# Rounded-type transposes for two tiles of each change of stage and for B's values, and a VectorE sum of squares at the end

## The chip, the cores and the metric

The kernel runs on one core of one Trainium2 chip. The metric is the device time of one launch in microseconds; the time of a kernel is the median of its runs. One further execution was recorded by the hardware profiler; all rows below come from that one.

## The reference, cut to what matters

One layer of an encoder on 1024 tokens of width 1024, in float32 (`D_FF` is 2816):

```python
h = x
h = h + 0.5 * swiglu(rms_norm(h, ffn1_norm), ffn1_w_gate, ffn1_w_up, ffn1_w_down)
u = rms_norm(h, mix_norm)
z = u @ w_in          # qA kA vA qB kB vB gA gB
ya = neighbourhood_attention_2d(qa, ka, va, na_rpb)
yb = windowed_gqa_sink(rope(qb), rope(kb), vb, sink_logit)
merged = sigmoid(ga) * (ya @ w_branch_a) + sigmoid(gb) * (yb @ w_branch_b)
h = h + merged @ w_out
h = h + 0.5 * swiglu(rms_norm(h, ffn2_norm), ffn2_w_gate, ffn2_w_up, ffn2_w_down)
out = rms_norm(h, final_norm)
...
def rms_norm(x, g):
    return x * rsqrt(mean(x * x, axis=-1) + EPS) * g
def swiglu(x, w_gate, w_up, w_down):
    return (silu(x @ w_gate) * (x @ w_up)) @ w_down
```

## The kernel before, in words

The residual h stays on chip as eight tiles of 128 tokens x 1024 columns, numbered 0 to 7; `res(t)` gives tile t, which lies in `fx` for t < 4 and in `fa` for the others. The sixth tile is number 5, the eighth number 7.

Large products are done with Strassen's scheme. Every float32 operand of a product is split into a rounded part and the rounded rest (type F32R): ACT writes the first by a cast (L95 for activations, L327 for weights), DVE the second by a subtraction (L98, L334). `mm3` then issues three rounded matmuls into one bank: high times high (L149), high times low (L153), low times high (L155). A transposed tile, however, is a float32 operand: `nc.tensor.transpose` with the float32 identity `ident`.

Between two matmul stages the residual is normed, transposed and split. That is `transition`, called here "change of stage", which stands in the kernel twice with the shown transposes: once from FFN1's down projection to the input projection (the first change, 584 to 668 us of the profile), once from the mixer's output projection to FFN2 (the second, up to 1295 us). It is a generator: its steps are laid between the matmuls of the stage that ends and of the stage that begins. For a tile t it does:

- `pre`: the residual's last eviction (DVE, L640) and a store of the tile to `h_d` (SP, L1127 in the first change, L1812 in the second).
- `normed`: ACT squares the tile and sums the squares (L127; the squares go to a scratch tile of tag `xs`), POOL adds eps (L130) and takes the power -1/2 (L131), DVE scales the tile into the same scratch tile (L133). The tag `xs` has two buffers.
- `turn_tile`, which is `to_strassen`: `turned` issues eight 128x128 transposes on PE (L142) into two PSUM banks of tag "d"; then ACT and DVE form Strassen's sums and their splits (L216 to L222, L95, L98). In the first change each tile of the second half also leaves a copy in DRAM (L225, L226).

Tile t + 1 is normed ahead of tile t's transposes. The order of the instructions on each engine comes from the scheduler of the framework, which sorts by its own model of readiness, except where `pin` holds an instruction to the place in which it is written. Each engine works its list in order, and a wait holds all that stands behind it; DMAs issued by SP and POOL stand in those engines' lists.

B's values (the V of the windowed attention) are read from DRAM into an `xs` tile by SP (`v_b`), transposed (`turn_v`, L1163, eight transposes) and split.

At the end, `rest(t)` sums the squares of the first half of final tile t (the second half's sum stands already in `st[:, 1:2]`), and `scale(t)` scales and stores it. For the last tile the eviction and the squares are done in two pieces of 256 columns (L640 and L1833), two POOL additions (L1846, L1849) join the sums, and POOL's power (L1850) follows.

## Time and profile before

| | |
|---|---|
| median of three runs | 1912.23 us (1911.99, 1912.38, 1912.23) |
| profiled execution | 1912.05 us |
| its span on the core | 1910.1 us |
| PE busy in the span | 1901.1 us |
| DVE / ACT / POOL busy | 1456.1 / 961.3 / 244.3 us |
| mean granted PE clock | 0.999 |

The span runs from the first to the last recorded instruction; 1.95 us of the execution's time lie around it. PE is TensorE's matmuls, PEld its weight loads, which run beside matmuls; DVE is VectorE, ACT ScalarE, POOL GpSimd, SP SyncE. A name such as `g` or `d` in a row is a PSUM bank of that tag, `xs`, `ws`, `ar`, `fa` and `fx` are tiles in SBUF. "[2.24 <-POOL st L131]" at a row's end means that the engine was idle for 2.24 us before it, until POOL's L131 was done.

### The profile page before, as it was taken

Reading aid. Unit: us, or ns where it says so; the run is one execution under the profiler, and the core shown is the slowest. Engines: PE = TensorE matmul, PEld = TensorE weight load, DVE = VectorE, ACT = ScalarE, POOL = GpSimd, SP = SyncE. Lnnn points to the kernel's source line nnn. Section 1 sums busy time; section 2 is a strip of 40 time slices with the busy share of each in tenths; the row PEclk is TensorE's granted clock in tenths of the full one; section 3 lists DMA queues with packets and bytes.
Section 4 is the critical chain, followed back from the end, with each engine's and each line's share of the span. In section 5 each row is a group of like instructions: output and inputs, shape, how many; then the busy total and the mean of one; then the engine's idle time right before and its main releaser. Section 6 shows DMA issues by size and latency. Waiting matters only on the chain.

```text
span 1910.1 us, 26150 instructions
## 1 busy us (share of the span) xinstructions
PE 1901.1 (100%) x9020; PEld 1595.1 (84%) x9020; DVE 1456.1 (76%) x2644; ACT 961.3 (50%) x1876; POOL 244.3 (13%) x453
## 2 busy tenths in 40 slices
PE   9999999999999999999999999999999999999998
PEld 8888888888888888898898888888888888888886
DVE  8988888868957788666888999789665566559664
ACT  7533545544446543444898885274333333344453
POOL 0011232210000112211112300010010001000011
PEclk9999999999999999999999999999999999999999
DMA  7256977887454367855647969653333323492341
GB/s 270 95 188 217 336 273 289 298 293 282 127 166 135 112 206 225 243 192 206 181 123 207 296 227 335 232 195 132 136 111 107 108 89 111 162 357 93 110 139 61
DMA packets 176963, 365.84 MB, mean 192 GB/s; under 512 B 17728, under 2 KB 75968, under 8 KB 176832
## 3 DMA queue, kind: packets, MB, share of 16 engines
q1 hardware_dynamic: 136784, 236.23, 37.6%
q0 software_dynamic: 39184, 126.90, 19.2%
q8 instruction: 71, 1.16, 0.3%
q10 hardware_dynamic: 864, 1.05, 0.2%
q14 instruction: 60, 0.49, 0.1%
HBM read 244.06 MB, written 121.83 MB: 192 GB/s over the span
## 4 chain that ended last, share of the span: by engine, by line
PE 96%; ACT 2%; DVE 1%; DMA 0%; issue 0%; SPq 0%; POOLq 0%; POOL 0%; DVEq 0%
PE g L149 18%; PE g L155 18%; PE g L153 18%; PE d L155 12%; PE d L149 12%; PE d L153 12%; PE d L1620 2%; PE g L1634 1%; PE d L1596 1%; PE d L1597 1%; PE g L1639 1%; PE d L142 1%; ACT fa L1604 0%; ACT ws L95 0%; DMA fx<-in_xt_dram 0%; DVE ws L98 0%
## 5 line engine op out<-in xcount | busy, mean ns | idle before, releaser
L149 PE MATMUL g<-ar,ws 128*128 128x512 f32 x1062 | 407.0, 393 | 0.2
L153 PE MATMUL g<-ar,ws 128*128 128x512 f32 x1062 | 403.8, 390 | 0.0
L155 PE MATMUL g<-ar,ws 128*128 128x512 f32 x1062 | 402.6, 390 | 0.0
L149 PE MATMUL d<-ar,ws 128*128 128x512 f32 x706 | 275.3, 390 | 0.0
L155 PE MATMUL d<-ar,ws 128*128 128x512 f32 x706 | 274.9, 389 | 0.1
L153 PE MATMUL d<-ar,ws 128*128 128x512 f32 x706 | 274.8, 389 | 0.0
L155 PEld LDWEIGHTS g<-ar,ws 128*128 128x128 f32 x1062 | 199.2, 188 | 41.8
L153 PEld LDWEIGHTS g<-ar,ws 128*128 128x128 f32 x1062 | 199.4, 188 | 40.7
L149 PEld LDWEIGHTS g<-ar,ws 128*128 128x128 f32 x1062 | 196.4, 188 | 37.1 <-ACT xs L1331 1.1
L334 DVE TENSOR_TENSOR ws<-raw,ws 128x512 fp32r<-128x512 f32 x216 | 147.6, 689 | 78.5 <-ACT ws L327 77.7
L327 ACT CAST ws<-raw 128x512 fp32r<-128x512 f32 x216 | 132.7, 620 | 143.1 <-PE g L155 61.2
L155 PEld LDWEIGHTS d<-ar,ws 128*128 128x128 f32 x706 | 132.5, 188 | 28.0 <-DVE ws L334 0.5
L153 PEld LDWEIGHTS d<-ar,ws 128*128 128x128 f32 x706 | 132.6, 188 | 27.7 <-DVE ar L1000 0.3
L149 PEld LDWEIGHTS d<-ar,ws 128*128 128x128 f32 x706 | 132.7, 188 | 27.1
L95 ACT CAST ws<-raw 128x512 fp32r<-128x512 f32 x88 | 54.9, 623 | 115.5 <-PE d L155 63.6
L98 DVE TENSOR_TENSOR ws<-raw,ws 128x512 fp32r<-128x512 f32 x88 | 60.5, 688 | 55.2 <-ACT ws L95 55.1
L95 ACT CAST ar<-raw 128x512 fp32r<-128x512 f32 (+1 forms) x80 | 52.1, 654 | 84.4 <-PE g L153 51.5
L446 POOL DMA_DIRECT2D hid<-fx x91 | 49.5, 544 | 343.2 <-DVE fx L506 221.6
L149 PE MATMUL g<-ws,ws 128*128 128x512 f32 x232 | 90.9, 392 | 0.0
L153 PE MATMUL g<-ws,ws 128*128 128x512 f32 x232 | 90.3, 389 | 0.0
L155 PE MATMUL g<-ws,ws 128*128 128x512 f32 x232 | 90.1, 390 | 0.0
L95 ACT CAST ws<-ar 128x512 fp32r<-128x512 f32 x104 | 64.3, 618 | 47.4 <-PE g L155 25.4
(382 smaller groups left out, 3878.7 us busy)
## 6 DMA issues: line engine op xcount, KB each, us to landing
raw<-hid SPq DMA_DIRECT2D x70, 512.0 KB
hid<-fx POOLq DMA_DIRECT2D x91, 256.0 KB, 2.9
ar<-in_ffn_w_down_dram SPq DMA_DIRECT2D x32, 512.0 KB
raw<-in_ffn_w_up_dram SPq DMA_DIRECT2D x31, 512.0 KB
wo_d<-made POOLq DMA_DIRECT2D x28, 512.0 KB, 4.6
raw<-in_ffn_w_gate_dram SPq DMA_DIRECT2D x27, 512.0 KB
hid<-fa POOLq DMA_DIRECT2D x51, 256.0 KB, 2.9
ar<-zs_d POOLq DMA_DIRECT2D x48, 256.0 KB, 9.3
```

Source lines behind the costliest of these rows:

```text
L95: hi = nc.scalar.copy(dst_hi, src)
L98: (eng or nc.vector).tensor_tensor(dst_lo, src, f32v(dst_hi), op=ALU.subtract)
L142: nc.tensor.transpose(pt[:, c * P:(c + 1) * P], xs[:, (half * 4 + c) * P:(half * 4 + c + 1) * P], ident)
L149: o = nc.tensor.matmul(b, lhs[0], r[0], start=first, stop=False, **kw)
L153: nc.tensor.matmul(b, lhs[0], r[1], start=False, stop=False, **kw)
L155: nc.tensor.matmul(b, lhs[1], r[0], start=False, stop=last, **kw)
L327: nc.scalar.copy(w[0][:, :512], a)
L334: nc.vector.tensor_tensor(w[0][:, 512:], a, f32v(w[0][:, :512]), op=ALU.subtract)
L446: nc.gpsimd.dma_start(hid[PRODUCTS.index(p), i], src)
L1596: nc.tensor.matmul(b[:, :nw], un["q"][s], un["kd"][s][:, k0 * P:k1 * P], start=True, stop=False)
L1597: nc.tensor.matmul(b[:, :nw], un["q"][s], un["kl"][s][:, k0 * P:k1 * P], start=False, stop=True)
L1620: nc.tensor.transpose(pt[:, i * P:(i + 1) * P], un["pr"][s][:, i * P:(i + 1) * P], ident)
```

## The change

Four edits, of which the first serves the others:

- `ident` is made as an F32R tile, by the two POOL instructions that the library call issued. Users that stay in float32 view it as such.
- In each change of stage, tiles 5 and 7 are normed as before into a tile y; then a POOL DMA copies y (128 x 1024, 512 KB, SBUF to SBUF) into a second tile x of tag `xs` and type F32R, and the eight transposes read x, with the output written as F32R. Since `xs` has two buffers, x takes the buffer of the previous tile, free after that tile's transposes, and the next tile's square takes y's buffer, free after the copy. That makes four copies and 32 transposes of the other type.
- `turn_v` transposes B's values in F32R (eight transposes); the tile is declared F32R and filled by the same SP DMA.
- For the very last tile, one eviction of 512 columns replaces two of 256, and one DVE instruction multiplies the half by itself and sums it, starting from `st[:, 1:2]`; POOL's power follows directly. The two ACT squares and two POOL additions are gone.

```diff
@@ -55,8 +54,10 @@
         uid[0] += 1
         return f"{s}_{uid[0]}"
-    ident = const.tile([P, P], F32, name="ident")
-    make_identity(nc, ident)
+    ident = const.tile([P, P], F32R, name="ident")
+    nc.gpsimd.memset(f32v(ident), 0.0)
+    nc.gpsimd.affine_select(out=ident, in_=f32v(ident), compare_op=ALU.not_equal, fill=1.0, base=0, pattern=[[-1, P]],
+                            channel_multiplier=1)
     nhalf4 = const.tile([P, 4], F32, name="nhalf")
     nc.gpsimd.memset(nhalf4, -0.5)
     nhalf = nhalf4[:, 0:1]
@@ -135,11 +136,11 @@
         return xs
     def turned(xs):
-        pts = []
+        i, pts = f32v(ident) if xs.dtype == F32 else ident, []
         for half in range(2):
             pt = bank("d")
             for c in range(4):
-                nc.tensor.transpose(pt[:, c * P:(c + 1) * P], xs[:, (half * 4 + c) * P:(half * 4 + c + 1) * P], ident)
+                nc.tensor.transpose(pt[:, c * P:(c + 1) * P].bitcast(xs.dtype), xs[:, (half * 4 + c) * P:(half * 4 + c + 1) * P], i)
             pts.append(pt.rearrange("p (c t) -> p c t", c=4))
         return pts
@@ -164,22 +165,29 @@
         return fx[t] if t < 4 else fa[:, (t - 4) * 1024:(t - 3) * 1024]
-    def transition(pre, gain, turn_tile, post, halves=1, ahead=2):
+    def transition(pre, gain, turn_tile, post, halves=1, ahead=2, moved=(5, 7)):
         h, xs = {}, {}
         n = NTT // halves
+
+        def norm(t):
+            x = y = normed(h.pop(t), gain)
+            if t in moved:
+                x = main.tile([P, 1024], F32R, tag="xs", bufs=2, name=nm_("moved"))
+                pin(nc.gpsimd.dma_start(f32v(x), y))
+            xs[t] = x, y
         for base in range(0, NTT, n):
             for t in (base, base + 1):
                 h[t] = pre(t)
-            xs[base] = normed(h.pop(base), gain)
+            norm(base)
             yield
             for t in range(base, base + n):
                 for k in range(t + 2, t + 1 + ahead) if base and t == base else (t + (ahead if base else 2),):
                     if k < base + n:
                         h[k] = pre(k)
                 if t + 1 < base + n:
-                    xs[t + 1] = normed(h.pop(t + 1), gain)
-                turn_tile(t, xs.pop(t))
+                    norm(t + 1)
+                turn_tile(t, *xs.pop(t))
                 if t:
                     post(t - 1)
                 yield
@@ -193,7 +201,7 @@
     kept = []
-    def to_strassen(t, xs):
+    def to_strassen(t, xs, spare):
         pa, pb = turned(xs)
         tt = t % 4
@@ -221,7 +229,7 @@
         nc.vector.tensor_tensor(x11, t2, x11, op=ALU.subtract)
         nc.vector.tensor_tensor(x21, x21, t2, op=ALU.subtract)
         if kept:
-            x12 = xs[:, :512] if t == NTT - 1 else main.tile([P, 512], F32, tag="s1", bufs=1, name=nm_("s1"))
+            x12 = spare[:, :512] if t == NTT - 1 else main.tile([P, 512], F32, tag="s1", bufs=1, name=nm_("s1"))
             nc.scalar.copy(x12.rearrange("p (c t) -> p c t", c=4), pa)
             nc.sync.dma_start(kept[0][t - 4], x12)
...
@@ -1152,15 +1160,15 @@
     def v_b():
         mix["vb"] = [new_fx(k, F32R).rearrange("p (t d) -> p t d", t=NTT) for k in (0, 1)]
-        mix["vr"] = xs4()
-        pin(nc.sync.dma_start(mix["vr"], z_d[17 * P:18 * P, :]))
+        mix["vr"] = main.tile([P, 1024], F32R, tag="xs", bufs=2, name=nm_("vr"))
+        pin(nc.sync.dma_start(f32v(mix["vr"]), z_d[17 * P:18 * P, :]))
     def turn_v():
         r = mix["vr"]
         for n in range(2):
             pt = bank("g")
             for i in range(4):
-                nc.tensor.transpose(pt[:, i * P:(i + 1) * P], r[:, (4 * n + i) * P:(4 * n + i + 1) * P], ident)
+                nc.tensor.transpose(pt[:, i * P:(i + 1) * P].bitcast(F32R), r[:, (4 * n + i) * P:(4 * n + i + 1) * P], ident)
             pt = pt.rearrange("p (b s d) -> p b s d", s=2, d=HD)
             for s in range(2):
                 v = mix["vb"][s][:, 4 * n:4 * n + 4, :]
...
@@ -1841,12 +1849,12 @@
     def rest(t):
         st = late[t][1]
         if t == NTT - 1:
-            square(t, QUARTERS[0], 3)
-            square(t, QUARTERS[1], 0)
-            nc.gpsimd.tensor_tensor(st[:, 1:2], st[:, 1:2], st[:, 3:4], op=ALU.add)
+            y, h = late[t][0], res(t)
+            nc.vector.tensor_tensor_reduce(out=y[:, LO], in0=h[:, LO], in1=h[:, LO], scale=1.0 / D, scalar=st[:, 1:2],
+                                           op0=ALU.mult, op1=ALU.add, accum_out=st[:, 0:1])
         else:
             square(t, LO, 0)
-        nc.gpsimd.tensor_tensor(st[:, 0:1], st[:, 0:1], st[:, 1:2], op=ALU.add)
+            nc.gpsimd.tensor_tensor(st[:, 0:1], st[:, 0:1], st[:, 1:2], op=ALU.add)
         nc.gpsimd.tensor_tensor(st[:, 2:3], st[:, 0:1], nhalf, op=ALU.pow)
     def scale(t):
@@ -1864,7 +1872,7 @@
         if n in (12, 13, 14, 15):
             begin(n - 8)
     for t in range(4, NTT):
-        down.tail(t - 4, QUARTERS[:2] if t == NTT - 1 else (LO,))
+        down.tail(t - 4)
         rest(t)
         if t > 4:
             scale(t - 1)
```

PE's number of instructions stays. In the rows below, a line of the kernel after stands 1 to 8 lines further down than in the kernel before (L127 becomes L128, L327 becomes L335, L1116 becomes L1124).

POOL's list in the first change, before: the eps and power steps of tiles 4 to 7 and then the stores of results to `z_d`.

```order
L130 TENSOR_SCALAR st_5288<-st_5288 128x1
L131 TENSOR_TENSOR st_5288<-st_5288,nhalf 128x1
L130 TENSOR_SCALAR st_5311<-st_5311 128x1
L131 TENSOR_TENSOR st_5311<-st_5311,nhalf 128x1
L130 TENSOR_SCALAR st_5392<-st_5392 128x1
L131 TENSOR_TENSOR st_5392<-st_5392,nhalf 128x1
L130 TENSOR_SCALAR st_5463<-st_5463 128x1
L131 TENSOR_TENSOR st_5463<-st_5463,nhalf 128x1
L1092 DMA z_d<-fa 128x512 x3
```

And after:

```order
L131 TENSOR_SCALAR st_5288<-st_5288 128x1
L132 TENSOR_TENSOR st_5288<-st_5288,nhalf 128x1
L131 TENSOR_SCALAR st_5311<-st_5311 128x1
L132 TENSOR_TENSOR st_5311<-st_5311,nhalf 128x1
L177 DMA moved_5316<-xs_5310 128x1024
L131 TENSOR_SCALAR st_5394<-st_5394 128x1
L132 TENSOR_TENSOR st_5394<-st_5394,nhalf 128x1
L131 TENSOR_SCALAR st_5465<-st_5465 128x1
L132 TENSOR_TENSOR st_5465<-st_5465,nhalf 128x1
L1100 DMA z_d<-fa 128x512 x2
L177 DMA moved_5470<-xs_5464 128x1024
L1100 DMA z_d<-fa 128x512
```

Tile 5's copy stands between the power of tile 5 and the eps of tile 6; tile 7's copy stands after two of the three stores to `z_d`.

ACT's list at the same place, before: the squares of tiles 4, 5 and 6 (L127, into `xs`), then splits of tile 4 (L95), the copy that goes to DRAM (L225), weights (L327) and an eviction (L1116).

```order
L127 ACTIVATE xs_5287,st_5288<-fa 128x1024
L127 ACTIVATE xs_5310,st_5311<-fa 128x1024
L127 ACTIVATE xs_5391,st_5392<-fa 128x1024
L95 CAST ar_5219<-fa 128x4x128
L95 CAST ar_5218<-fa 128x4x128
L95 CAST ar_5220<-d_5321 128x4x128
L225 COPY s_609_5336<-d_5316 128x512
L327 CAST ws_5250<-raw_5228 128x512
L1116 ACTIVATE fa<-g_5339 128x512
```

And after:

```order
L128 ACTIVATE xs_5287,st_5288<-fa 128x1024
L128 ACTIVATE xs_5310,st_5311<-fa 128x1024
L96 CAST ar_5219<-fa 128x4x128
L233 COPY s_610_5338<-d_5318 128x512
L96 CAST ar_5218<-fa 128x4x128
L96 CAST ar_5220<-d_5323 128x4x128
L96 CAST ar_566<-fx_75 128x4x128
L335 CAST ws_5250<-raw_5228 128x512
L1124 ACTIVATE fa<-g_5341 128x512
L128 ACTIVATE xs_5393,st_5394<-fa 128x1024
L1124 ACTIVATE fa<-g_5355 128x512
```

The square of tile 6 has moved from directly behind that of tile 5 to behind the splits, the copy, the weights' cast and one eviction.

DVE's list in the second change, before: an eviction of the projection that ends (L640), the first difference of tile 4 (L216), the scaling of tile 6 (L133), and the rest of tile 4's sums.

```order
L640 SCALAR_TENSOR_TENSOR fa<-g_11388,fa 128x512
L216 TENSOR_TENSOR fa<-d_11924,fx_11171 128x512
L133 SCALAR_TENSOR_TENSOR xs_11983<-fa,st_11984,gain_11308 128x1024
L218 TENSOR_TENSOR fa<-d_11929,fa 128x512
L98 TENSOR_TENSOR ar_5219<-fa,ar_5219 128x4x128
L221 TENSOR_TENSOR fx_11171<-fa,fx_11171 128x512
L98 TENSOR_TENSOR ar_11175<-fa,ar_11175 128x4x128
L98 TENSOR_TENSOR ar_11734<-d_11929,ar_11734 128x4x128
L222 TENSOR_TENSOR fx_11171<-fx_11171,fa 128x512
```

And after:

```order
L648 SCALAR_TENSOR_TENSOR fa<-g_11392,fa 128x512
L224 TENSOR_TENSOR fa<-d_11930,fx_11175 128x512
L346 TENSOR_TENSOR raw_11763<-s_1765_12218,raw_11763 128x512
L226 TENSOR_TENSOR fa<-d_11935,fa 128x512
L99 TENSOR_TENSOR ar_5219<-fa,ar_5219 128x4x128
L229 TENSOR_TENSOR fx_11175<-fa,fx_11175 128x512
L99 TENSOR_TENSOR ar_11179<-fa,ar_11179 128x4x128
L99 TENSOR_TENSOR ar_11738<-d_11935,ar_11738 128x4x128
L230 TENSOR_TENSOR fx_11175<-fx_11175,fa 128x512
L134 SCALAR_TENSOR_TENSOR xs_11989<-fa,st_11990,gain_11312 128x1024
```

The scaling of tile 6 has moved from the third of these rows to the last, behind all of tile 4's sums, and a subtraction for weights (L346) stands in its old place.

More of the change, by code (lines that the diff above doesn't have):

```diff
@@ L7 @@
 from concourse import mybir
-from concourse.masks import make_identity
 from concourse._compat import with_exitstack
@@ L918, in keep_busy @@
             k = i % 4 * P
-            nc.tensor.transpose(b[:, k:k + P], ident, ident)
+            nc.tensor.transpose(b[:, k:k + P], f32v(ident), f32v(ident))
     def first_stage():
@@ L985, in do @@
                 for k in range(4):
-                    nc.tensor.transpose(r[i][:, k * P:(k + 1) * P], st[i][0][:, k:k + 1].to_broadcast([P, P]), ident)
+                    nc.tensor.transpose(r[i][:, k * P:(k + 1) * P], st[i][0][:, k:k + 1].to_broadcast([P, P]), f32v(ident))
             elif op == "stat":
@@ L1619, in turn @@
             for i in range(nk):
-                nc.tensor.transpose(pt[:, i * P:(i + 1) * P], un["pr"][s][:, i * P:(i + 1) * P], ident)
+                nc.tensor.transpose(pt[:, i * P:(i + 1) * P], un["pr"][s][:, i * P:(i + 1) * P], f32v(ident))
             if len(un["v"]) == 2:
```

## Prediction

> **What bounds the kernel now.** The page comes first: its busy lines, then the chain that ended last.
>
> ```profile
> span 1910.1 us, 26150 instructions
> PE 1901.1 (100%) x9020; PEld 1595.1 (84%) x9020; DVE 1456.1 (76%) x2644; ACT 961.3 (50%) x1876; POOL 244.3 (13%) x453
> PE 96%; ACT 2%; DVE 1%; DMA 0%; issue 0%; SPq 0%; POOLq 0%; POOL 0%; DVEq 0%
> ```
>
> PE is busy in 1901.1 of 1910.1 us. So two kinds of thing move the time: what PE's own instructions take, and whatever makes PE wait. Both must be looked for at the places of the edit. Next I read PE's timeline at a transposed tile, at B's values, and at a product that is not rounded.
>
> ```profile
> 584.64 0.39 PE L155 MATMUL g<-ws,ws 128*128 128x512 f32 x1
> 584.86 1.03 PE L142 MATMUL d<-ident,xs 128*128 128x128 f32 x8
> 585.65 0.47 PE L149 MATMUL g<-ws,ws 128*128 128x512 f32 x1
> ...
> 809.77 0.28 PE L155 MATMUL d<-ws,ar 128*128 128x256 f32 x1
> ...
> 810.98 1.03 PE L1163 MATMUL g<-ident,xs 128*128 128x128 f32 x8
> ...
> 13.52 2.05 PE L974 MATMUL g<-ones,xs 128*128 128x128 f32 x16
> 15.32 0.48 PE L149 MATMUL d<-ar,ws 128*128 128x512 f32 x1
> ```
>
> Columns: start, duration, instruction. Durations overlap, so the price of one is the distance between starts. Eight transposes take 585.65 - 584.86 = 0.79 us, 99 ns each. A rounded product of 512 columns takes 584.86 - 584.64 = 0.22 us. Ten rounded products of 256 columns stand between 809.77 and 810.98, 0.121 us each. At 13.52 stand eight full-precision 128-wide products, two passes each: 1.80 / 8 = 0.225 us for one.
>
> **The change, part by part.** *1. Forty transposes in the rounded type* (four tiles of eight, and B's values). No row shows a rounded instruction of 128 columns. Upper end: 0.121 us, that of the 256-wide one, a loss of 40 x 0.022 = 0.9 us. Lower end: 512 to 256 columns saves 0.10 us, so 256 to 128 saves about 0.054, an estimate: 0.067 us, a gain of 40 x 0.032 = 1.3 us. The weights of a rounded product also load longer than those of today's transposes:
>
> ```profile
> L142 PEld LDWEIGHTS d<-ident,xs x128: 137/140/144, 584.6 to 1294.5; 128*128 128x128 f32 x128
> L155 PEld LDWEIGHTS g<-ar,ws 128*128 128x128 f32 x1062 | 199.2, 188 | 41.8
> ```
>
> (140 ns against 188; loads overlap, so this is no pitch by itself). I take 80 ns, nearer the extrapolation than the middle, since the width is what the rows say sets the pitch, with something left for the loads: -40 x 0.019 = -0.8 us.
>
> [...]
>
> *2. The tail.* Today's last tile, from the last matmul:
>
> ```profile
> 1899.74 0.69 DVE L640 SCALAR_TENSOR_TENSOR fa<-g,fa 128x512 f32<-128x512 f32 x1 [0.27 <-PE g L155]
> ...
> 1903.14 0.76 DVE L640 SCALAR_TENSOR_TENSOR fa<-g,fa 128x256 f32<-128x256 f32 x2 [0.26 <-PE g L155]
> 1903.60 0.42 ACT L1833 ACTIVATE raw<-fa 128x256 f32<-128x256 f32 x1 [0.75 <-DVE fa L640]
> ...
> 1904.65 0.19 POOL L1849 TENSOR_TENSOR st<-st 128x1 f32<-128x1 f32 x1 [0.27 <-ACT raw L1833]
> 1904.92 0.55 POOL L1850 TENSOR_TENSOR st<-st,nhalf 128x1 f32<-128x1 f32 x1
> ...
> L1601 DVE CUSTOM_DVE_ANT_0 fa<-d,fa x32: 530/540/559, 1026.8 to 1134.5; 128x384 f32<-128x384 f32 x32
> L1601 DVE CUSTOM_DVE_ANT_0 fa<-d,hs x10: 403/406/426, 1048.8 to 1142.3; 128x256 f32<-128x256 f32 x10
> L1601 DVE DVE_READ_ACCUMULATOR2_ANT nmx<- x128: 71/76/88, 919.5 to 1142.7; 128x1 f32 x128
> ```
>
> The pow starts at 1904.92 now, 1.78 us after the eviction began. After: one 512-wide eviction, 0.69 (row at 1899.74, back-to-back 0.60); a reduction whose nearest rows are the softmax's custom reductions, 540 ns at 384 columns and 406 at 256, so about 0.67 at 512; the read, 0.08; then a hop to POOL, between 0.12 and 0.33 us as in the rows above. Sum 1.48 to 1.77. The tail shrinks by 0 to 0.3; I take -0.25 us, since DVE feeds itself and the hop alone is unsure. All of it is on the path, which nothing covers at the end.
>
> *3. The first change of stage* (tile 4 is turned at 639.91; in the same timeline tile 5 at 651.02, tile 6 at 656.02, tile 7 at 666.64). Tile 5 is copied. The copy needs tile 4's slot (its transposes end at 639.91 + 1.03 = 640.94) and the scaled tile 5 (DVE, 640.37 + 1.28 = 641.65). So POOL issues it at about 641.7. Tile 6's square writes the slot that the copy reads, so it waits for the landing, and with it its whole chain.
>
> ```profile
> 639.91 1.03 PE L142 MATMUL d<-ident,xs 128*128 128x128 f32 x8
> ...
> 642.37 1.06 ACT L127 ACTIVATE xs<-fa 128x1024 f32<-128x1024 f32 x1 [3.00 <-DVE fa L640]
> ...
> 645.93 0.61 ACT L1116 ACTIVATE fa<-g 128x512 f32<-128x512 f32 x1
> ...
> 643.91 0.89 POOL L131 TENSOR_TENSOR st<-st,nhalf 128x1 f32<-128x1 f32 x1
> ...
> 640.37 1.28 DVE L133 SCALAR_TENSOR_TENSOR xs<-fa,st,gain 128x1024 f32<-128x1024 f32 x1 [2.24 <-POOL st L131]
> ...
> 647.29 1.28 DVE L133 SCALAR_TENSOR_TENSOR xs<-fa,st,gain 128x1024 f32<-128x1024 f32 x1
> ...
> 657.15 1.28 DVE L1120 SCALAR_TENSOR_TENSOR fa<-g,fa 128x512 f32<-128x512 f32 x2
> ...
> 657.89 0.50 PE L149 MATMUL g<-ar,ws 128*128 128x512 f32 x1
> ```
>
> The copy's price: no row copies SBUF to SBUF. The nearest are POOL's other transfers of 512 KB, in a stretch with room and in one that is full:
>
> ```profile
> ar<-wo_d POOLq DMA_DIRECT2D x6, 512.0 KB, 3.5
> ar<-wo_d POOLq DMA_DIRECT2D x2, 512.0 KB, 8.1
> ...
> 640.00:644.00 4.00, 4.00 (x24) 3.42 (x23) 3.50 (x5) 1.64 (x4) 0.65 (x3) 1.00 0.30 121
> 1270.00:1274.00 4.00, 4.00 (x23) 3.38 (x22) 4.00 (x7) 1.86 (x4) 0.87 (x2) 1.00 1.00 336
> 1274.00:1278.00 4.00, 4.00 (x19) 3.33 (x18) 4.00 (x7) 3.50 (x7) 0.00 (x0) 1.00 0.86 305
> ```
>
> (columns of the windows: busy time of PE, PEld, DVE, ACT, POOL, then the clock, the DMA share and GB/s). At 640 the DMA engines are 0.30 busy, so I take 3.5 to 4: landing near 645.5. The square now stands behind the rows of ACT that ended at 645.93 + 0.61 = 646.54; without its 1.06 ahead of them they end about 645.5 to 646.1. The square then starts near 646.1; from a square's start to POOL's result took 644.80 - 642.37 = 2.43 us, or 2.1 with the usual 0.57 us pow. DVE can scale tile 6 at 648.3 to 648.6 and does it at 647.29 now: it waits 1.0 to 1.3 us. DVE then stays busy without a gap to the evictions at 657.15, and PE's matmul at 657.89 starts as the first of those ends, with no slack. So the wait reaches PE: ends 0 (if the copy lands by 644) and 1.3, taken as +1.1 us. The square is all that the copy holds on ACT; behind it there stand an eviction and casts that waited anyway. Tile 7's copy is issued behind two stores on POOL, has nothing after it in the slot, and must land by 666.64: tile 7 is scaled at 658.35 to 659.63, so 659.7 + 4 leaves 3 us. Its cost is 0.
>
> *4. The second change of stage.* Tile 5 is scaled by 1270.54, its copy goes out about 1271.5, into full DMA engines (1.00, then 0.86 above).
>
> ```profile
> 1271.50 1.06 ACT L127 ACTIVATE xs<-fa 128x1024 f32<-128x1024 f32 x1 [0.79 <-issue]
> 1274.39 0.62 ACT L327 CAST ws<-ahead 128x512 fp32r<-128x512 f32 x1 [1.74 <-DMA ahead<-in_ffn_w_gate_dram]
> ...
> 1274.07 1.27 DVE L133 SCALAR_TENSOR_TENSOR xs<-fa,st,gain 128x1024 f32<-128x1024 f32 x1
> ...
> 1278.09 1.03 PE L142 MATMUL d<-ident,xs 128*128 128x128 f32 x8
> ...
> 1292.15 0.61 DVE ws L334
> 1292.80 0.50 PE d L155
> ```
>
> Landing at 1275.0 (3.5) to 1279.6 (8.1). Tile 5's transposes want it at 1278.09: late by 0 to 1.5. Tile 6's square stood at 1271.50 and now waits for the landing; its scaling by DVE is placed about five rows later than 1274.07, near 1278.9. At the middle landing, 5.8 us, 1277.3, the scaling is ready at 1277.3 + 2.3 = 1279.6: DVE waits 0.7. At 8.1 it waits 3.0. ACT's casts already wait for weights (1.74 above), and 512 KB more in these queues makes those later. DVE lies on the chain here up to the cast's difference at 1292.15 that PE takes at 1292.80, so its wait costs PE in full. Ends 0 and 3.0; I take the middle landing, +0.7 us. Tile 7's copy has 1293.84 - 1286.8 = 7 us for its 3.5 to 4.6: 0.
>
> Everything else goes at 0: the identity's type, the tile names, the reading of B's values by the same transfer.
>
> **Sum.** -0.8 - 0.25 + 1.1 + 0.7 = +0.75 us on the profiled execution's 1912.05 us: 1912.8. The median of the runs is 1912.23, 0.18 above that execution: 1913.0.
>
> **The rivals.**
> *A. The copies hide.* Both land in 2 to 3 us and DVE's waits vanish; the 0.30 share at 640 speaks for it, the full window at 1270 against. With the extrapolated 67 ns: 1912.23 - 1.3 - 0.25 = 1910.7.
> *B. The copies land late* (slower). Landings as in the full stretch, 8.1 us, at both places: tile 6 of the first change is scaled at 641.7 + 8.1 + 2.3 = 652.1, 4.8 us after 647.29, and the second change waits 3.0. 1912.23 - 1.05 + 7.8 = 1919.0. It counts as slower from a landing of about 6.3 us at both places (then 3.0 + 1.2 of waits, and the transfers that it delays). For it: some POOL transfers take longer still,
>
> ```profile
> ar<-zs_d POOLq DMA_DIRECT2D x48, 256.0 KB, 9.3
> ```
>
> though in another pattern; against it the 0.30 at 640.
> *C. Rounded transposes run like full products*, 0.225 us: 40 x 0.126 = +5.0 in place of -0.8, 1918.8. Against it: every other rounded instruction here is quicker than a full one.
> *D. The type buys nothing*: 99 ns stays. 1912.23 - 0.25 + 1.8 = 1913.8. [...]
>
> **How the numbers follow.** 0.2% (3.8 us) is about what a measurement of this kernel can tell from no change; the bounds are 1908.4 and 1916.1. Forecast 0.53, A 0.20, B 0.12, C 0.04, D 0.08, and 0.03 that an unseen shift of the schedule gains more than the -1.3 and -0.25 allow. Faster 0.03; same 0.53 + 0.20 + 0.08 = 0.81; slower 0.16. The range runs from 1910.0 (A with the hop at its best and a slightly quicker pitch) to 1917.0, which leaves out most of B and C.
>
> **What would show it.** Right: the distance from the first moved transpose to the next matmul falls from 0.79 to about 0.64 us; tile 5's copies take 3.5 to 6 us; tile 6's scaling waits for POOL's pow about 1 us; PE shows a gap near 658 and one near 1293; the last pow starts 0.2 us sooner after the last matmul. Wrong: a pitch of 99 ns or more, copies that land in 8 us, or no gap on DVE before tile 6's scaling. What would upset all of it is a changed order elsewhere that opens a gap on PE outside these stretches.

## The result, and the profile after

The changed kernel takes 1917.95 us in the median of 11 runs (1915.31 to 1926.62); the kernel before takes 1913.12 us in 11 runs beside it (1911.99 to 1918.19). The ratio is 1.003, with a 95% interval of 1.0015 to 1.0044: it is slower, by 3 to 8 us. The profiled execution took 1917.1 us.

The page of the changed kernel: the span, the busy times, and the shares of the chain that ended last.

```profile
span 1915.2 us, 26160 instructions
PE 1901.3 (99%) x9020; PEld 1593.3 (83%) x9020; DVE 1456.7 (76%) x2645; ACT 958.9 (50%) x1872; POOL 246.1 (13%) x455
PE 93%; ACT 2%; DVE 2%; DMA 1%; issue 1%; POOL 0%; SPq 0%; POOLq 0%; DVEq 0%; ACTq 0%
```

PE is as busy as before (1901.3 us against 1901.1), and the span is 5.1 us longer: PE does not do more, it waits more. The list of what PE waited for (engine, line, releaser; us in total, times, longest) names the places. Before it had one row, the start:

```profile
PE g L919 <- POOL ident masks.py:199: 1.5, 1, 1.5
```

After:

```profile
PE d L143 <- DMA moved<-xs: 1.6, 1, 1.6
PE g L927 <- POOL ident L59: 1.5, 1, 1.5
PE d L1604 <- DVE nmx L1609: 1.5, 1, 1.5
PE g L150 <- ACT ar L96: 0.6, 1, 0.6
PE g L150 <- DVE fa L1128: 0.4, 1, 0.4
PE g L150 <- DVE fa L648: 0.4, 1, 0.4
PE d L154 <- DVE ar L1008: 0.3, 1, 0.3
```

The first row is tile 7's copy in the second change of stage, at 1298 us. The third is in the attention, at 1102 us, in code that the diff does not touch. The fourth is in the second change, at 1286 us, and the next two in the first change, at 660 and 654 us. Measured from the usual distance between matmuls, these places lose 1.75, 1.66, 0.78, 0.58 and 0.58 us, 5.35 in all. The last row, at 9.8 us, loses 0.47 us and is not the edit's: run 13 below, whose program differs from the kernel before only in the attention, loses 0.56 us there. Less the 1.0 us that the transposes and the tail gain, that makes 4.8 of the 5.1 us.

The engines' timelines of the changed kernel, in order of time:

```profile
649.13 1.28 DVE L134 SCALAR_TENSOR_TENSOR xs<-fa,st,gain 128x1024 f32<-128x1024 f32 x1 [1.33 <-POOL st L132]
...
651.53 0.79 PE L143 MATMUL d<-ident,moved 128*128 128x128 f32 x8
652.16 0.46 PE L150 MATMUL g<-ar,ws 128*128 128x512 f32 x1
...
654.18 0.47 PE L150 MATMUL g<-ar,ws 128*128 128x512 f32 x1 [0.42 <-DVE fa L648]
...
659.60 0.50 PE L150 MATMUL g<-ar,ws 128*128 128x512 f32 x1 [0.42 <-DVE fa L1128]
...
1101.15 0.42 DVE L1572 TENSOR_TENSOR fa<-g,s 64x256 f32<-64x256 f32 x1 [1.85 <-DMA y_d<-fa]
...
1102.09 0.44 PE L1604 MATMUL d<-ar 128*128 128x384 f32 x1 [1.51 <-DVE nmx L1609]
...
1274.36 0.62 POOL L177 DMA_DIRECT2D moved<-xs  x1 [2.53 <-DVE ws L342]
...
1279.50 0.59 ACT L487 COPY fa<-g 128x512 f32<-128x512 f32 x1
...
1279.98 1.06 ACT L128 ACTIVATE xs<-fa 128x1024 f32<-128x1024 f32 x1
...
1282.49 1.29 DVE L134 SCALAR_TENSOR_TENSOR xs<-fa,st,gain 128x1024 f32<-128x1024 f32 x1 [0.77 <-POOL st L132]
...
1286.32 0.47 PE L150 MATMUL g<-ar,ws 128*128 128x512 f32 x1 [0.62 <-ACT ar L96]
...
1290.90 1.28 DVE L134 SCALAR_TENSOR_TENSOR xs<-fa,st,gain 128x1024 f32<-128x1024 f32 x1
...
1292.74 0.53 POOL L177 DMA_DIRECT2D moved<-xs  x1 [0.82 <-issue]
...
1298.04 0.84 PE L143 MATMUL d<-ident,moved 128*128 128x128 f32 x8 [1.59 <-DMA moved<-xs]
...
1908.14 0.69 DVE L648 SCALAR_TENSOR_TENSOR fa<-g,fa 128x512 f32<-128x512 f32 x1 [0.27 <-PE g L156]
...
1909.71 0.55 POOL L1858 TENSOR_TENSOR st<-st,nhalf 128x1 f32<-128x1 f32 x1 [2.62 <-DVE st L1853]
```

Eight transposes in the rounded type take 652.16 - 651.53 = 0.63 us, 79 ns each (99 before). Tile 6's scaling waits 1.33 us in the first change and 0.77 us in the second, where ACT squares tile 6 at 1279.98, directly behind another of its instructions (L487). Tile 7's scaling in the second change starts at 1290.90, its copy goes out at 1292.74, and the transposes start with its landing. At the end the eviction to the power takes 1909.71 - 1908.14 = 1.57 us, against 1.78 before. The copies' issue to landing, in the list of DMAs of two stretches (the first change, then the second):

```profile
moved<-xs POOLq DMA_DIRECT2D x2, 512.0 KB, 3.9
...
moved<-xs POOLq DMA_DIRECT2D x2, 512.0 KB, 5.3
```

### The profile page after: what moved, and what is told of

Same layout as the page of the kernel before. It is cut to its first block, busy times and chain, and to the rows that moved or that the text cites. A ratio compares the mean times of both kernels' runs of the same rounds, so it can differ in the third digit from the quotient of the medians.

```text
span 1915.2 us, 26160 instructions
## 1 busy us (share of the span) xinstructions
PE 1901.3 (99%) x9020; PEld 1593.3 (83%) x9020; DVE 1456.7 (76%) x2645; ACT 958.9 (50%) x1872; POOL 246.1 (13%) x455
## 3 DMA queue, kind: packets, MB, share of 16 engines
q8 instruction: 71, 1.16, 0.2%
## 4 chain that ended last, share of the span: by engine, by line
PE 93%; ACT 2%; DVE 2%; DMA 1%; issue 1%; POOL 0%; SPq 0%; POOLq 0%; DVEq 0%; ACTq 0%
PE g L150 17%; PE g L156 17%; PE g L154 17%; PE d L156 12%; PE d L150 12%; PE d L154 12%; PE d L1628 1%; DMA y_d<-fa 1%; PE g L1642 1%; PE d L1604 1%; PE d L1605 1%; PE g L1647 1%; ACT fa L1612 0%; PE d L143 0%; ACT ws L96 0%
## 5 line engine op out<-in xcount | busy, mean ns | idle before, releaser
L342 DVE TENSOR_TENSOR ws<-raw,ws 128x512 fp32r<-128x512 f32 x216 | 147.9, 689 | 77.0 <-ACT ws L335 76.0
L335 ACT CAST ws<-raw 128x512 fp32r<-128x512 f32 x216 | 132.7, 620 | 139.0 <-PE g L156 61.0
L96 ACT CAST ws<-raw 128x512 fp32r<-128x512 f32 x88 | 54.8, 623 | 117.7 <-PE d L156 61.6
L454 POOL DMA_DIRECT2D hid<-fx x91 | 49.3, 542 | 344.8 <-DVE fx L514 231.5
L96 ACT CAST ar<-raw 128x512 fp32r<-128x512 f32 (+1 forms) x80 | 52.2, 655 | 81.9 <-PE g L154 51.5
L96 ACT CAST ws<-ar 128x512 fp32r<-128x512 f32 x104 | 64.2, 618 | 49.2 <-PE g L156 25.4
```

The costliest lines, as they stand in the source:

```text
L96: hi = nc.scalar.copy(dst_hi, src)
L335: nc.scalar.copy(w[0][:, :512], a)
L342: nc.vector.tensor_tensor(w[0][:, 512:], a, f32v(w[0][:, :512]), op=ALU.subtract)
L454: nc.gpsimd.dma_start(hid[PRODUCTS.index(p), i], src)
```

## The experiments

All were compared with the kernel before, run beside them on the same chip. "Loss" is the distance of a PE start from the usual one, as above. The median of the kernel before was 1912.77 us beside the runs 1 to 4, 1912.47 beside 5 to 8, 1912.65 beside 9 to 12, 1912.47 beside 13 to 16 and 1912.68 beside 17 and 18.

**1. The changed kernel once more** (the same instructions).

> The changed kernel itself once more, for a second profile. Theory T (the loss is made of the waits that the four copies add: about 1.0 us on PE in the first change of stage and 2.4 us in the second, while the 1.7 us gap in the attention at 1102 us of the first profile is chance of a DMA and not of the edit): 1914.5 to 1917 us, PE gaps again near 654, 660, 1286 and 1298 us, none at 1102. Rival R (the attention's gap belongs to the edit): 1917 to 1919, with a gap of 1.5 us or more in the attention again.

Median 1921.42 us (1914.98 to 1922.76), ratio 1.0035 (1.0025 to 1.0045). The profiled execution, the fastest at 1914.98, loses 0.58 and 0.55 us in the first change, 1.70 before tile 7 in the second, and 0.71 in the attention. So tile 7's wait and those of the first change come again; the wait at 1286 us shrinks to 0.2 us, though tile 6's scaling waits the same 0.77 us; and the attention's wait has another size. Neither theory is right as it stands: the gap in the attention is neither absent nor constant, and the median lies above both.

**2. No tile moved.**

```diff
-    def transition(pre, gain, turn_tile, post, halves=1, ahead=2, moved=(5, 7)):
+    def transition(pre, gain, turn_tile, post, halves=1, ahead=2, moved=()):
```

> No tile is moved in either change of stage: no copies, and only B's eight values are transposed in the rounded type; the tail is the new one. Theory T: -8 x 0.02 - 0.25 = -0.4 us against before, that is level with it, and no PE gap in either change of stage beyond those of before. Rival U (the new tail, or the identity in the rounded type, costs something by itself): 2 us or more over before.

Median 1912.37 us (1911.68 to 1917.09), ratio 0.9996 (0.9987 to 1.0005), no added wait in either change of stage. Level with before, as theory T had it; the tail and the identity cost nothing that can be seen.

**3. and 4. Both tiles moved in one change of stage only.**

```diff
 # 3: the call of the second change
-    merge.into(transition(down2, gain, to_strassen, behind(hg), 2, 3), hg)
+    merge.into(transition(down2, gain, to_strassen, behind(hg), 2, 3, ()), hg)
 # 4: the call of the first change
-    down.into(transition(down1, gain, to_strassen, behind(pg, (0, 1)), 2), pg)
+    down.into(transition(down1, gain, to_strassen, behind(pg, (0, 1)), 2, moved=()), pg)
```

> Tiles 5 and 7 are moved in the first change of stage alone (24 transposes in the rounded type with B's values). Theory T: +1.0 of waits - 24 x 0.02 - 0.25 = +0.3 us against before. Rival R: as much over before as the whole change, +4 or more, since the attention lies behind the first change. Rival U: +2 or more.

> Tiles 5 and 7 are moved in the second change of stage alone (24 transposes in the rounded type with B's values). Theory T: +2.4 of waits - 24 x 0.02 - 0.25 = +1.7 us against before, PE gaps near 1286 and 1298 as in the changed kernel. Rival R: about 0, as nothing that runs ahead of the attention has changed.

First alone: 1915.5 us (1913.71 to 1918.8), ratio 1.0014 (1.0005 to 1.0023), +2.7 us where T expected +0.3; losses of 0.53 and 0.57 us in the first change and 2.41 in the attention. Second alone: 1914.58 us (1913.75 to 1919.4), ratio 1.0011 (1.0002 to 1.002), +1.8 us where T expected +1.7; losses of 0.80 and 1.77 us in the second change, none in the attention. The first change's price is not only its own two gaps. The second's profile showed something that no theory had: the windows around tile 7's wait (busy times of PE, PEld, DVE, ACT, POOL, then the granted clock).

```profile
1290.00:1294.00 4.00, 3.99 (x17) 2.67 (x15) 4.00 (x8) 3.62 (x7) 0.54 (x1) 1.00 0.84 296
1294.00:1296.00 2.00, 0.40 (x5) 0.43 (x5) 2.00 (x4) 1.96 (x5) 0.00 (x0) 1.00 0.16 64
1296.00:1297.00 1.00, 1.00 (x9) 0.91 (x8) 1.00 (x3) 0.44 (x2) 0.00 (x0) 0.90 0.29 98
1297.00:1300.00 3.00, 3.00 (x9) 2.33 (x8) 3.00 (x6) 2.32 (x4) 0.00 (x0) 0.50 0.85 313
1300.00:1301.00 1.00, 1.00 (x6) 0.78 (x5) 1.00 (x2) 0.01 (x1) 0.00 (x0) 0.89 1.02 391
```

PE idles 1.6 us, resumes, and a microsecond later its clock is 0.50 for some 3.4 us: 9 matmuls in 3 us where 13 fit. The clock lost is 0.10 + 3 x 0.50 + 0.11 = 1.7 us, more than the wait itself. The changed kernel's profile has the same wait at 1298 without it (granted clock 1.00 from 1290 to 1303 us).

**5. to 8. One tile moved in one change of stage** (the `moved` argument of that call is `(7,)` or `(5,)`, that of the other call `()`).

```diff
 # 5
+    merge.into(transition(down2, gain, to_strassen, behind(hg), 2, 3, (7,)), hg)
 # 6
+    merge.into(transition(down2, gain, to_strassen, behind(hg), 2, 3, (5,)), hg)
 # 7
+    down.into(transition(down1, gain, to_strassen, behind(pg, (0, 1)), 2, moved=(5,)), pg)
 # 8
+    down.into(transition(down1, gain, to_strassen, behind(pg, (0, 1)), 2, moved=(7,)), pg)
```

> Only tile 7 of the second change of stage is moved (16 transposes in the rounded type with B's values). Theory T2 (tile 7's copy is late in the changed kernel only because tile 5's copy pushes tile 7's scaling on DVE back by some 5 us): the copy has its 7 us, PE does not wait before tile 7's transposes, 16 x 0.02 + 0.25 = 0.6 us faster than before. Rival V (tile 7's copy is late by itself, since it goes out behind a store on POOL): PE idle about 1.6 us ahead of tile 7's transposes, +1 us against before, or more where the granted clock falls after it.

> Only tile 5 of the second change of stage is moved. Theory T2: one PE gap of about 0.8 us near 1284 us (ACT's split is late, with tile 6's square behind the copy) and DVE late by 1 to 3 us up to tile 7: +0.8 - 0.6 = +0.2 us against before. Rival V: half of what the second change's two copies cost, about the same.

> Only tile 5 of the first change of stage is moved. Theory T2: the two PE gaps of 0.55 us near 653 and 659 us, so +1.1 - 0.6 = +0.5 us against before in the changes of stage, and beyond that the attention's stall near 1101 us, which the runs with the first change's copies showed (0.7 to 2.4 us) and those without did not; +1 to +2.5 us in all. Rival W (the attention's stall comes from tile 7's copy or is chance): +0.5 us and no PE wait near 1101 us.

> Only tile 7 of the first change of stage is moved. Theory T2: no wait near 653 to 668 us, 0.6 us faster than before. If the attention's stall goes with the delay of the program it is absent; rival W: PE waits 0.7 us or more near 1101 us and the kernel is 1 us or more slower than before.

Five: 1913.08 us (1911.71 to 1917.93), ratio 1.0004 (0.9995 to 1.0012). Its timelines, of DVE, POOL and PE:

```profile
1285.95 1.27 DVE L134 SCALAR_TENSOR_TENSOR xs<-fa,st,gain 128x1024 f32<-128x1024 f32 x1
...
1287.80 0.62 POOL L177 DMA_DIRECT2D moved<-xs  x1 [5.15 <-PE d L143]
...
1294.32 0.80 PE L143 MATMUL d<-ident,moved 128*128 128x128 f32 x8
```

Without tile 5's copy, tile 7 is scaled at 1285.95, its copy is out at 1287.80, and PE does not wait. Theory T2 holds for the wait, rival V falls: tile 7's copy is late in the changed kernel because of tile 5's. (Here the copy stands ahead of a store on POOL's list, L454, that precedes it in the changed kernel. But there the store's issue ended at 1291.92, before tile 7 was scaled at 1292.18, so it did not hold the copy.) The gain of 0.6 us does not show in the times: the median is 0.6 us above that of the kernel before, and three of eleven executions lie at 1915.9 to 1917.9. The profile loses 0.64 us in the attention.

Six: 1913.38 us (1912.55 to 1915.47), ratio 1.0001 (0.9992 to 1.0009), a loss of 0.98 us at 1284 us and, at 1295 us, 0.55 us idle behind DVE's split of weights (L342); +0.9 us in the median, inside what cannot be told from none.

Seven: 1919.07 us (1913.81 to 1921.95), ratio 1.0027 (1.0017 to 1.0036). The executions fall in two groups, four at 1913.8 to 1914.7 and seven at 1917.7 to 1922. The profile, of 1914.69, has 0.58 and 0.56 us in the first change and 2.03 us in the attention. Both theories priced the low group; neither the high one, of which there is no profile.

Eight: 1912.57 us (1911.67 to 1919.22), ratio 1.0008 (0.9999 to 1.0017), no wait in the first change, 0.39 us in the attention, three of eleven executions at 1917.9 or more.

**9. Only a delay**: nothing moved, but tile 5 of the first change is transposed twice.

```diff
-        pa, pb = turned(xs)
+        pa, pb = turned(xs, 2 if kept and t == 5 else 1)
```

> No tile is moved (as in the second experiment), but tile 5 of the first change of stage is transposed twice (8 transposes more, 0.79 us of PE). It tells what starts the attention's stall. Theory D (the delay of PE by some 0.8 us is enough: the attention then meets its transfers in another phase): many executions at 1917 us and above with a lower clock, as with tile 5's copy alone (7 of 11). Rival K (the copy or the order that it brings is needed): all but one or two executions at 1912.4 + 0.8 = 1913.2 us, 1 in 7 above 1916 as in the kernel before.

1913.53 us (1912.62 to 1915.27), ratio 1.0 (0.9992 to 1.0009). Ten of eleven within 1912.6 to 1914: the delay is paid and no more, rival K. (The eleventh is the profiled one, with 2.11 us lost in the attention.) A later program alone does not bring the high group. But the wait in the attention needs no copy: here, where nothing is moved, DVE's row has it too.

```profile
1101.38 0.42 DVE L1572 TENSOR_TENSOR fa<-g,s 64x256 f32<-64x256 f32 x1 [2.30 <-DMA y_d<-fa]
```

**10. The copies by SP.**

```diff
-                pin(nc.gpsimd.dma_start(f32v(x), y))
+                pin(nc.sync.dma_start(f32v(x), y))
```

> The whole change, but the four copies are issued by SP instead of POOL. Theory P (POOL's way of issuing is slow: about 0.6 us to issue and 3.9 to 5.3 us to land): copies land in 2.5 to 3.5 us, the waits near 654, 659 and 1298 us shrink by 1 us each, and the kernel gains 1.5 to 2.5 us on the changed one. Rival Q (the transfer itself takes the time, and SP's list holds the copy behind stores and loads that wait): 1917 to 1921 us as the changed kernel.

1918.65 us (1914.6 to 1921.09, 7 runs), ratio 1.0027 (1.0016 to 1.0038). The first change's losses are 0.59 and 0.55 us, as with POOL. In the second change PE does not wait ahead of tile 7's transposes, as theory P had it, but it loses 0.45 and 1.42 us at 1288 and 1290 us and idles 0.49 us behind L342: SP issues tile 5's copy at 1278.77, right after a store at 1278.35, 2.6 us after tile 4's transposes ended (1276.19). The time is rival Q's, and SP's list did hold a copy; how long the copies took to land by SP is not on record. The attention loses 2.18 us, and the clock falls to 0.50 behind it.

**11. A wider gap**: the second change alone, tile 7 copied twice.

```diff
-                pin(nc.gpsimd.dma_start(f32v(x), y))
+                for _ in range(1 + (t == 7)):
+                    pin(nc.gpsimd.dma_start(f32v(x), y))
```

> The second change alone, with tile 7's copy issued twice, so that PE waits some 3 to 4 us longer ahead of tile 7's transposes. Theory G (an idle PE has its clock halved for about 3.4 us when the pause is long enough; 1.6 us was enough in one profile of three): the granted clock falls to 0.5 behind this gap in nearly every execution, so that the kernel costs 3.5 us of wait and 1.7 us of clock over the second change alone: 1914.6 + 5.2 = 1919.8 us, clock 0.998. Rival H (the fall was chance and has nothing to do with the pause): 1918.1 us at clock 0.999.

1918.32 us (1916.53 to 1921.71, 6 runs), ratio 1.0029 (1.0018 to 1.0041). The edit did less than was expected: the loss ahead of tile 7's transposes is 2.57 us, 0.8 more than in number 4 and not 3 to 4 more, and 1.38 us are lost just before. The clock is at 0.50 behind the longer wait. The attention, too, loses 1.89 us, without any copy in the first change. One execution of six had a mean clock of 1.000, so the fall is not certain behind such a pause; the three at 0.999 tell nothing, since the profiled one, where the fall is seen, is one of them. Neither G nor H is shown.

**12. Tile 7 alone, in both changes** (`moved=(7,)`).

> Tile 7 alone is moved, in both changes of stage; B's values and the tail as in the change (24 transposes in the rounded type). Theory T2: neither copy is waited for; 24 x 0.02 + 0.25 = 0.73 us faster than before in undisturbed executions, 1911.7 us; that is the best that the edit can give. Rival V: 1 us or more slower than before.

1913.64 us (1911.53 to 1919.05), ratio 1.0006 (0.9996 to 1.0017). Three executions at 1911.5 to 1911.8, as T2 had it, and four at 1916.9 or more. Its profile shows the attention's wait from its cause to PE:

```profile
1100.33 0.42 DVE L1572 TENSOR_TENSOR fa<-g,s 64x256 f32<-64x256 f32 x1 [2.27 <-DMA y_d<-fa]
...
1101.28 0.44 PE L1604 MATMUL d<-ar 128*128 128x384 f32 x1 [1.92 <-DVE nmx L1609]
```

The attention collects a head pair's results in `fa`, and SP stores them to `y_d`. The next head pair's first write to the place waits until the store has landed; DVE's list stands behind that write, and with it the softmax and PE. The store runs in a stretch where the DMA engines are full, in the kernel before as well (windows, the DMA share is the last but one number):

```profile
1095.00:1100.00 5.00, 5.00 (x35) 4.64 (x34) 4.63 (x17) 4.12 (x11) 2.31 (x4) 1.00 1.18 253
```

and in the changed kernel:

```profile
1095.00:1100.00 5.00, 5.00 (x35) 4.53 (x34) 3.94 (x14) 4.01 (x11) 2.26 (x3) 1.00 1.25 284
```

**13. to 16. The same values stored in two halves, each as soon as it is complete**, so that the write that waits meets a store issued two units earlier; in the kernel before, the changed one, number 7 and number 12.

```diff
-                        if j in (3, 7):
-                            nc.sync.dma_start(y_d[512 + hp * P:512 + (hp + 1) * P, cols].rearrange("(s p) t -> p s t", s=2), both)
+                        if j % 2:
+                            k = j % 4 // 2 * 256
+                            c0 = j // 4 * 512 + k
+                            nc.sync.dma_start(y_d[512 + hp * P:512 + (hp + 1) * P, c0:c0 + 256].rearrange("(s p) t -> p s t", s=2),
+                                              both[:, :, k:k + 256])
```

> The kernel before, with the attention's results of three head pairs stored in two halves of 256 columns, each as soon as it is complete, so that the write that reuses the place waits for a store that went out two units (some 6 us) earlier. Theory S (the late landing of that store is the seat of the high executions): no execution above 1914.5 us, median 1912.2. Rival: 1 in 7 executions above 1915.5 us as in the kernel before.

> The changed kernel with the same early stores. Theory S: 1914.5 to 1917 us, the upper ones with a halved clock behind tile 7's wait in the second change; no PE wait near 1101 us; median 1915.3, 3 us or more under the changed kernel. Rival: 1917 to 1922 us as before.

> Tile 5's copy in the first change alone, with the same early stores. Theory S: all executions between 1913 and 1914.5 us (before +1.1 of gaps - 0.6), where seven of eleven were at 1917.7 to 1922 without the early stores. Rival: the same spread up to 1922 us.

> Tile 7 alone moved in both changes, B's values and the tail as in the change, with the same early stores: what is left of the edit when every wait that it adds is taken away. Theory S: 1911.5 to 1912.5 us, median 1911.7, a faster kernel than both. Rival: 1911.5 to 1919 us as without the early stores.

Thirteen: 1913.11 us (1911.95 to 1914.79), ratio 0.9999 (0.999 to 1.0008); none above 1914.8, while 5 of the 32 executions of the kernel before beside it were at 1915.6 to 1916.9. The median is not better: the store's wait is a matter of some executions.

Fifteen: 1913.59 us (1912.74 to 1915.37), ratio 1.0003 (0.9995 to 1.0012). The high group is gone: 0 of 11 above 1915.4, where number 7 had 7 of 11 above 1917.6. This is the clearest of the runs: theory S holds for tile 5's copy in the first change. (It ran on another chip than number 7; the kernel before has the same median, 1912.47, beside both.)

Sixteen: 1912.4 us (1911.6 to 1915.61), ratio 1.0 (0.9991 to 1.0008). Number 12's four executions from 1916.9 on are gone, but the profile, of 1915.31, has another wait in the attention, 3.16 us at 1114 us, for weights (`ws<-wb_d`). No profile without the early stores has a wait there; 17 and 18 have it again. Not measurably faster than before: nothing that was run beats the kernel before beyond the measurement.

Fourteen: 1918.15 us (1915.01 to 1921.06, 10 runs), ratio 1.0025 (1.0015 to 1.0035). Five stay at 1915 to 1917.1 and five at 1919.2 to 1921.1 with mean clocks of 0.997 to 0.998. Theory S is half right here: without the store's wait (none in the profile) the whole change keeps a high group.

**17. and 18. With the early stores: the second change alone, and the whole change less tile 7's copy in the second.**

```diff
 # 17
+    down.into(transition(down1, gain, to_strassen, behind(pg, (0, 1)), 2, moved=()), pg)
 # 18
+    merge.into(transition(down2, gain, to_strassen, behind(hg), 2, 3, (5,)), hg)
```

> Tiles 5 and 7 moved in the second change alone, with the early stores. Theory C (the wait for tile 7's copy is the seat, by the clock): two groups, 1913.5 to 1914.5 us at 0.999 and 1916 us or more at 0.998, the second at least 3 of 11. Rival: all executions within 1913.5 to 1915 us, so that the high ones need the first change's copies too.

> The whole change but tile 7's copy in the second change, with the early stores (three copies stay, and the tail). Theory C: all executions between 1914 and 1915.5 us (before +1.1 in the first and +0.8 in the second change, - 0.7), clock 0.999. Rival: half of them at 1918 us and above as with all four copies.

Seventeen: 1916.5 us (1914.22 to 1922.43), ratio 1.0018 (1.0009 to 1.0027). Seven of eleven are at 1916 or more, so the first change's copies are not needed for high executions. (Number 4, the same without the early stores, had two of eleven there, on another chip: for this kernel the early stores are no help.) The profile is of the slowest, 1922.43 us, mean clock 0.997. PE's rows in the attention, and the windows behind tile 7's wait in the second change:

```profile
1115.63 1.19 PE L150 MATMUL g<-ar,ws 128*128 128x512 f32 x2 [3.93 <-DMA ws<-wb_d]
1116.63 1.05 PE L154 MATMUL g<-ar,ws 128*128 128x512 f32 x2
...
1301.74 0.84 PE L143 MATMUL d<-ident,moved 128*128 128x128 f32 x8 [1.66 <-DMA moved<-xs]
...
1303.00:1304.00 1.00, 1.00 (x4) 0.80 (x3) 1.00 (x3) 0.62 (x1) 0.00 (x0) 0.54 0.83 268
1304.00:1305.00 1.00, 1.00 (x4) 0.71 (x3) 1.00 (x3) 0.73 (x2) 0.00 (x0) 0.50 0.82 283
1305.00:1306.00 1.00, 1.00 (x4) 0.81 (x3) 1.00 (x3) 0.90 (x2) 0.00 (x0) 0.50 1.00 393
1306.00:1307.00 1.00, 1.00 (x5) 0.83 (x4) 1.00 (x3) 0.09 (x1) 0.00 (x0) 0.75 1.02 393
```

This execution shows what made it a high one: a wait for weights in the attention (3.93 us) with a slow clock behind it (two 512-wide matmuls from 1115.63 take 1.00 us, against 0.46 at the usual pitch), and tile 7's wait (1.66) with another fall of 0.46 + 0.50 + 0.50 + 0.25 = 1.7 us.

Eighteen: 1914.58 us (1914.2 to 1918.35), ratio 1.0011 (1.0003 to 1.002). Seven of eleven within 1914.2 to 1914.8, three at 1915.9 to 1916.6, one at 1918.35. Against fourteen's five of ten at 1919 or more: tile 7's late copy carries most of the high group, as theory C has it, though a few high executions are left; the profile of one, 1915.94 us, has 2.03 us lost in the attention behind DVE.

Over the nineteen profiles beside that of the kernel before, PE lost 1.6 us or more at one place sixteen times. Until the last matmul, the clock fell to 0.5 at five of them and nowhere else.

## Why the prediction was wrong

*Term 1, the transposes: right.* 79 ns against the 80 forecast (upper end 121, lower end 67); 40 x 0.020 = 0.8 us gained. Rivals C (0.225 us each) and D (99 ns) are out.

*Term 2, the tail: right.* 1.78 to 1.57 us, -0.21 against -0.25.

*Term 3, the first change: right at its place.* Landing 4.0 us (forecast 3.5 to 4), DVE's wait 1.33 us (1.0 to 1.3), PE's two losses 1.16 us (+1.1), though half of it comes at 654 us, at a matmul that the prediction did not name; tile 7's copy free, as run 8 confirms.

*Term 4, the second change: the step that failed.* "Tile 7's copy has 1293.84 - 1286.8 = 7 us for its 3.5 to 4.6: 0" took tile 7's scaling from the trace of before. Its rows, before and, last, after:

```profile
1270.37 1.04 PE L142 MATMUL d<-ident,xs 128*128 128x128 f32 x8
...
1285.47 1.27 DVE L133 SCALAR_TENSOR_TENSOR xs<-fa,st,gain 128x1024 f32<-128x1024 f32 x1
...
1273.03 1.04 PE L143 MATMUL d<-ident,xs 128*128 128x128 f32 x8
```

In the changed order the scaling stands behind two more rows on DVE, and behind everything that tile 5's copy made late there: it starts at 1290.90 instead of 1285.47, 5.4 us later where the program as a whole is 2.7 us later (tile 4 is transposed at 1273.03 instead of 1270.37). The copy lands after 5.2 us and PE loses 1.75 us. Run 5 gives tile 7 its old place and the loss is gone. (Even there the copy goes out at 1287.80 and not at 1286.8, since it also needs the place of tile 6, which is transposed until 1287.3.) Rival B had the sign but not the place: the copies did not take 8.1 us.

The rest of the term came out near its number, in part by luck. Tile 5's copy took 5.5 us (5.8 forecast), DVE waited 0.77 us (0.7) and PE lost 0.78 us. But the copy had landed at 1274.36 + 5.5 = 1279.86, before ACT came to tile 6's square (1279.98): the square's new place in ACT's list set the wait at least as much as the landing did, and the wait is 0.77 us in each of eight profiles with POOL's copy, for landings from 4.9 to 6.1 us. And PE's loss is not at the weights' split near 1293 but at 1286, behind ACT's cast of tile 5's sums (L96); it is 0.2 us in runs 1 and 14 and 0.4 to 1.2 us in the six others.

*What no term had.* First, the clock: a wait on PE was priced at its length, and a loss of 1.6 us or more brought a further 1.7 us in five of sixteen cases. Second, the attention: the prediction named "a changed order elsewhere that opens a gap on PE outside these stretches" as what would upset it, but gave it no place and no price. A stretch with full DMA engines (a share of 1.18 before, 1.25 after) has waits of 0 to 4 us that differ between executions, and with tile 5's copy in the first change high executions are more frequent (above 1915.5 us: 7 of 11 in run 7, none in run 6, 16 of 143 in the kernel before beside the runs). Runs 7 and 15 show that they then hang on the store to `y_d`; runs 14, 17 and 18 that tile 7's late copy in the second change carries a second part.

In sum, the forecast of +0.75 us becomes: -0.8, -0.2, +1.2 and +0.8, all near their forecast, and +1.75 for tile 7, together +2.75, not far from the distance between the fastest executions (1914.98 against 1911.63, 3.4 us). The rest of the measured 5 us is put down to the two unpriced things, which come in some executions and not in others; most of the high executions were not profiled, so this part is argued and not shown.

Left open: why the copies of the first change make high executions more frequent. Run 9 rules out the delay as the whole cause; POOL's queue is not needed either (run 10). The lists of SP and DVE in the input projection also change with those copies, and that was not tried apart.

## What to carry to other kernels

When a change moves instructions, take the slack of every later step from the new order and the new times, not from the old trace: the second copy had 7 us in the old place and less than none in the new one. Ask, too, what the new order alone does: an instruction that moves back in its engine's list can be held longer by that list than by the transfer, as tile 6's square was here (the copy landed at 1279.86, the square started at 1279.98). On a kernel whose TensorE is busy all the time, price a wait like the sixteen here (a loss of 1.6 us or more) at its length plus a chance of losing 1.7 us of clock (five of the sixteen), and look for stretches with full DMA engines far from the edit: in the one here, with a share of 1.18 to 1.25, the waits differed by 0 to 4 us between executions. Compare several executions before a wait that one profile shows is put down to the edit.

## What the runs showed of the hardware

The granted clock of TensorE fell to 0.5 at pauses of 1.61 us (run 4), 1.66 and 3.93 us (run 17), 2.01 us (run 10) and 2.41 us (run 11). Each time some 1.7 us were lost, in run 4 0.10 + 3 x 0.50 + 0.11 = 1.71, which is 3.4 us at 0.50. Eleven other pauses, from 1.51 us (the changed kernel, at 1102 us) to 2.99 us (run 16), left the clock at 1.00. So length alone does not sort these sixteen, and what does was not shown.

A copy of 512 KB within SBUF, issued by POOL, took 3.4 to 4.0 us from issue to landing in the first change and 4.9 to 6.1 us in the second (3.7 for the repeated copy of run 11). The DMA share over the copy does not explain the difference (in the changed kernel 0.78 and 0.76 in the first change, 0.97 and 0.69 in the second, for 4.0, 3.9, 5.5 and 5.2 us), and the reason stays open. Issuing it from SP left PE's losses in the first change as they were (0.59 and 0.55 us against 0.58 and 0.58); that says little of the transfer, since in the changed kernel, too, ACT came to tile 6's square at 646.98, after the landing (642.71 + 4.0).
